# Moving the second mixer's eight modulation slots into the two feed-forward blocks before and after it

## The chip, the cores and the metric

The kernel runs on one core of one Trainium2 chip. The metric is the device time of one execution in microseconds; three runs are given by their median and their ends. One more execution was recorded by the hardware profiler, and all rows of the profile come from that one.

The engines are named as in the profile: PE is TensorE's matmul, PEld its weight load, DVE is VectorE, ACT is ScalarE, POOL is GpSimd, SP is the queue that issues most loads from HBM.

## The reference, cut to what matters

The model is a chain of three transformer layers over 512 latent tokens (and 256 context tokens, in the first two), width 1024, all in float32. Each layer is a mixer (attention beside a pooling and a convolution branch in the first two layers, attention beside a linear recurrence in the third) followed by a gated feed-forward block. Every layer is steered by a modulation vector that depends on the condition vectors `c` and `c_ctx` alone, not on the tokens:

```python
def adaln(cond, w_mod, b_mod):
    m = jnp.dot(jax.nn.silu(cond), w_mod) + b_mod
    return jnp.split(m[..., None, :], 6, axis=-1)
...
sh1, sc1, g1, sh2, sc2, g2 = adaln(c, w_mod[l], b_mod[l])
h = modulate(rms_norm(x, norm1_g[l]), sh1, sc1)
...
x = x + g1 * jnp.einsum('blm,md->bld', mix, w_out[l])
x = x + g2 * swiglu(modulate(rms_norm(x, norm2_g[l]), sh2, sc2), w_ffn_in[l], w_ffn_out[l])
```

`w_mod` is 1024 by 6144 for each layer, so the three modulations read 72 MB and hold 6 parts (two shifts, two scales, two gates) of 1024 numbers for each of two conditions. A layer's parts are needed at different times: the first shift and scale at its first norm, the first gate at the mixer's output projection, the second shift and scale at the norm before the feed-forward block, and the second gate inside that block.

## The kernel before, in words

**Slots.** The modulation work is cut into 72 slots, 24 for each layer, of 256 columns of `w_mod` each. They are used in one fixed order, the list `mods` (all slots of layer 0, then of layer 1, then of layer 2); this text counts them from 0 to 71. `mod_slot` is one of them. It takes 1 MB of weights, which `Weights.next` loads in two halves of 512 KB into buffers named `raw`. Eight calls of matmul (line 343; each appears in the profile as two records, so a slot has 16) multiply the conditions with the weights, 32 columns of the array at a time, into a PSUM tile. Then `post` copies the tile to SBUF on ACT (line 349), and `post2` transposes it twice on PE (line 354) into another PSUM tile, reduces that on DVE (line 356), and adds bias and gain on DVE (lines 358 and 362). `mod_slot` gets a tag that says which PSUM banks it takes: "pj" (two banks, shared with the projections) in the mixers, "ap" (two other banks) in the feed-forward blocks. Ahead of the first slot of layer 2, which is slot 48, `cond` (line 332) computes the conditions of that layer on ACT.

**Where the slots are issued.** Eight slots go with the start of the first mixer. `MODS_MIX` says how many each of the first two mixers issues within its windows (lists of work items that `windows` writes out and `layer` spreads over the steps of the attention); `MODS_FFN` says how many follow each of the 22 hidden blocks of a feed-forward block in `ffn`, through `mod_fill`. Before, that is 12 slots in the first mixer (8 to 19), 22 in the first feed-forward block (20 to 41, one to a hidden block), 8 in the second mixer (42 to 49), and 22 in the second feed-forward block (50 to 71). The third feed-forward block has none.

**Weights.** All other weights come through a second stream of the same class. A load of 1 MB comes in two halves into the same `raw` buffers, of which there are four; each half is then split into a high part (`whi`, ACT, line 229) and a low part (`wlo`, POOL, line 230). Both streams load one entry ahead of the one in use. So a slot whose weights are there, but which has not run, holds two of the four `raw` buffers.

**Matmuls.** Each projection is three matmuls for one product (lines 254, 257 and 258 in `mm3`). A hidden block of a feed-forward block is 16 such triples of 512 columns (in the first one also 16 of 256 columns for the context), then an ACT Silu (line 953), a product on DVE (line 954) and a split.

**The mixer's other work.** In the second mixer DVE runs 62 taps of a convolution over 512 columns (line 664, `conv_taps`), the maxima of the softmax (line 799), its weighted difference (line 844) and parts of the pooling branch (lines 639 to 644). PE transposes queries and keys (line 791, in `qk_turn`) into a "pj" bank, from an operand that POOL finishes (line 782). `conv_ln` normalises the convolution: sums on PE (lines 676 and 306), a power on POOL (line 297), a spread on PE (line 322).

**Order.** The program is written in one order, and the framework's scheduler sorts each engine's queue by the written order and its own estimate of times. On the chip each engine runs its queue in that order.

Of the kernel before, what the change touches and what calls it, by code (L numbers as in the profile page):

```python
# [24 lines left out]
NJ = FF // 128  # L25
# [216 lines left out]
class K:  # L242
# [463 lines left out]
        return post(g, ps)  # L706


    MODS_MIX = [(4, 8, 0, 0), (2, 4, 2, 0)]
    MODS_FFN = [[1] * NJ, [1] * NJ, [0] * NJ]  # L710

    LAST = [(0, 0, 0.2, 0.4, 0.6, 0.8, 1), (0, 0.1, 0.4, 0.7, 1)]
    SLOT = {"g": 0, "u": 1, "p": 2, "v0": 3, "q0": 4, "q1": 5, "v1": 6, "q2": 7, "q3": 8}
# [1 line left out]
    def windows(self, l):  # L715
# [22 lines left out]
        q0, v0 = tm("q0"), tm("v0")  # L738
        nm = self.MODS_MIX[l]
        conv = [it for g in ("01", "2") for n in "gu" for it in fm(n) if it[2] in g]  # L740
# [180 lines left out]
    def ffn(self, l, pf, hx, hc, xt, xc, then, at=None):  # L921
# [5 lines left out]
        for gi, (j0, jn, cn) in enumerate(DOWN[l]):  # L927
            gt = []
            for j in range(j0, j0 + jn):
# [28 lines left out]
                gt.append((gh, gl))  # L958
                self.mod_fill(self.MODS_FFN[l][j], "ap", j == j0 + jn - 1)
                if at and j in at:  # L960
# [788 lines left out]
```

## Time and profile before

| | us |
|---|---|
| median of 3 runs | 2637.24 |
| lowest and highest | 2633.56, 2638.14 |
| the profiled execution, its own time | 2634.79 |
| its span, first to last instruction | 2632.9 |
| PE busy in it | 2500.2 (95%) |
| DVE, ACT, POOL busy in it | 954.6, 907.7, 1143.8 |

The profiled execution is 2.45 us below the median of the runs and lies within them. Times within it are counted from the span's start. The first mixer ends and the first feed-forward block begins near 460 us; the second mixer lies from about 1030 to 1390 us, the second feed-forward block from there to about 1775 us, and the third one from about 2255 us to the end.

Matmuls are pipelined, so one record is longer than the step from one start to the next; a busy PE in a stretch says that it never waited, not how fast it went.

### The profile page before, as it was taken

The page shows a single profiled execution, that of the slowest core. Times are in us where ns is not written, and L with a number is a line of the kernel's source. Part 1 is how long each engine was busy: PE and PEld are TensorE (multiplying, and loading weights), DVE is VectorE, ACT ScalarE, POOL GpSimd, SP SyncE. Part 2 cuts the span into 40 slices and gives each one's busy share as a digit, 9 for nine tenths or more (in the row PEclk, how much of TensorE's full clock was granted, in tenths as well). Part 3 has the DMA queues.
Part 4 walks back from the last instruction along what each step waited for, and adds up shares of the span by engine and source line. Part 5 has one row for each costly group of instructions (what it writes and reads, how often), then busy time and mean ns, then how long its engine had stood idle before and what let it go on. Part 6 is the DMA issues. An engine that isn't in the chain of part 4 may idle for free.

```text
span 2632.9 us, 38646 instructions
## 1 busy us (share of the span) xinstructions
PE 2500.2 (95%) x15840; PEld 2131.1 (81%) x15840; DVE 954.6 (36%) x1932; ACT 907.7 (34%) x1905; POOL 1143.8 (43%) x965
## 2 busy tenths in 40 slices
PE   7889989999999999999999999999998898999998
PEld 5778869988888889877788777778887788888887
DVE  4896464121120123488542112113322756210112
ACT  4334543322122124333534223234443543422222
POOL 4544324433333334655326545454322344555553
PEclk9889989999999999999999999999998999999999
DMA  7113311323323233222324435343111021222221
GB/s 253 50 49 110 116 72 40 121 81 113 96 96 102 91 99 101 78 65 81 97 80 145 160 128 160 120 160 104 49 33 51 17 97 49 81 96 97 96 92 53
DMA packets 68961, 248.55 MB, mean 94 GB/s; under 512 B 7472, under 2 KB 10800, under 8 KB 67120
## 3 DMA queue, kind: packets, MB, share of 16 engines
q1 hardware_dynamic: 64992, 231.11, 26.9%
q10 hardware_dynamic: 3792, 14.97, 1.5%
q8 instruction: 125, 2.05, 0.3%
q14 instruction: 52, 0.43, 0.0%
HBM read 239.75 MB, written 6.29 MB: 93 GB/s over the span
## 4 chain that ended last, share of the span: by engine, by line
PE 48%; DVE 5%; ACT 2%; POOL 2%; issue 1%; DMA 1%; POOLq 0%; DVEq 0%; ACTq 0%
PE s2t L254 6%; PE s2t L258 6%; PE s2t L257 6%; PE pj L254 5%; PE pj L257 5%; PE pj L258 5%; PE ap L819 2%; DVE mix L664 1%; PE ap L254 1%; PE ap L257 1%; PE ap L258 1%; POOL wlo L230 1%; PE s2t L1531 1%; PE s2t L836 1%; PE ap L343 1%
## 5 line engine op out<-in xcount | busy, mean ns | idle before, releaser
L230 POOL TENSOR_TENSOR wlo<-raw,whi 128x512 fp32r<-128x512 f32 x576 | 745.4, 1326 | 700.5 <-ACT whi L229 700.2
L229 ACT CAST whi<-raw 128x512 fp32r<-128x512 f32 x576 | 319.5, 615 | 675.2 <-PE pj L257 248.1
L254 PE MATMUL s2t<-hh,whi 128*128 128x512 f32 (+1 forms) x1184 | 448.9, 380 | 0.8 <-ACT whi L229 0.8
L257 PE MATMUL s2t<-hl,whi 128*128 128x512 f32 (+1 forms) x1184 | 446.2, 377 | 1.8 <-POOL hl L428 1.8
L258 PE MATMUL s2t<-hh,wlo 128*128 128x512 f32 (+1 forms) x1184 | 447.5, 378 | 0.1
L254 PE MATMUL pj<-hh,whi 128*128 128x256 f32 (+1 forms) x1088 | 337.2, 312 | 8.5 <-ACT hh L425 2.9
L257 PE MATMUL pj<-hl,whi 128*128 128x256 f32 (+1 forms) x1088 | 331.5, 305 | 3.5 <-DVE hl L430 2.4
L258 PE MATMUL pj<-hh,wlo 128*128 128x256 f32 (+1 forms) x1088 | 331.1, 305 | 0.3 <-POOL wlo L230 0.3
L954 DVE TENSOR_TENSOR sg<-sg,s2t 128x512 f32<-128x512 f32 x66 | 45.4, 688 | 651.8 <-ACT sg L953 651.8
L257 PEld LDWEIGHTS s2t<-hl,whi 128*128 128x128 f32 x1184 | 223.0, 189 | 47.0 <-POOL hl L428 2.9
L258 PEld LDWEIGHTS s2t<-hh,wlo 128*128 128x128 f32 x1184 | 223.1, 188 | 46.9 <-issue 1.2
L254 PEld LDWEIGHTS s2t<-hh,whi 128*128 128x128 f32 x1184 | 222.4, 188 | 46.3 <-issue 2.1
L254 PEld LDWEIGHTS pj<-hh,whi 128*128 128x128 f32 x1088 | 210.4, 194 | 25.1 <-ACT hh L425 4.0
L327 POOL TENSOR_TENSOR gl<-sg,gh 128x512 fp32r<-128x512 f32 (+1 forms) x66 | 97.7, 1481 | 293.4 <-ACT gh L326 293.4
L257 PEld LDWEIGHTS pj<-hl,whi 128*128 128x128 f32 x1088 | 211.0, 194 | 12.4 <-DVE hl L430 2.6
L258 PEld LDWEIGHTS pj<-hh,wlo 128*128 128x128 f32 x1088 | 209.6, 193 | 8.5 <-POOL wlo L230 0.5
L254 PE MATMUL pj<-whi,hh 128*128 128x256 f32 x672 | 196.9, 293 | 1.3 <-ACT v L699 0.9
L257 PE MATMUL pj<-wlo,hh 128*128 128x256 f32 x672 | 194.4, 289 | 0.0
L258 PE MATMUL pj<-whi,hl 128*128 128x256 f32 x672 | 193.9, 289 | 0.0
L893 DVE SCALAR_TENSOR_TENSOR xt<-pj,mod,xt 128x256 f32<-128x256 f32 x224 | 101.6, 480 | 175.6 <-PE pj L258 175.1
L258 PE MATMUL pj<-gh,wlo 128*128 128x512 f32 (+1 forms) x400 | 145.6, 364 | 0.0
L254 PE MATMUL pj<-gh,whi 128*128 128x512 f32 (+1 forms) x400 | 145.5, 366 | 0.0
(382 smaller groups left out, 4464.7 us busy)
## 6 DMA issues: line engine op xcount, KB each, us to landing
raw<-in_w_mod SPq DMA_DIRECT2D x144, 512.0 KB, 4.0
raw<-in_w_up SPq DMA_DIRECT2D x132, 512.0 KB, 3.9
raw<-in_w_dn SPq DMA_DIRECT2D x66, 512.0 KB, 4.0
raw<-in_w_in SPq DMA_DIRECT2D x60, 512.0 KB, 3.9
raw<-in_w_out SPq DMA_DIRECT2D x24, 512.0 KB, 3.9
xt<-xs ACTq DMA_DIRECT2D x4, 1024.0 KB, 5.7
xt<-in_xT ACTq DMA_DIRECT2D x2, 1024.0 KB, 7.9
xs<-xt SPq DMA_DIRECT2D x2, 1024.0 KB, 3.8
```

What stands on the lines that cost most here:

```text
L229: nc.scalar.copy(out=h, in_=raw[:, q])
L230: nc.gpsimd.tensor_tensor(out=lo[:, s][:, q], in0=raw[:, q], in1=h.bitcast(F32), op=ALU.subtract)
L254: i = mm(ps, lhsT=lh, rhs=rh, start=start, stop=False)
L257: mm(ps, lhsT=lh, rhs=rl, start=False, stop=False)
L258: return mm(ps, lhsT=ll, rhs=rh, start=False, stop=stop)
L327: (lo_eng or self.nc.vector).tensor_tensor(out=lo, in0=src, in1=hi.bitcast(F32), op=ALU.subtract)
L343: nc.tensor.matmul(ps[g:g + 32], lhsT=self.cond_t[:, k, :], rhs=raw[k // 4][:, k % 4, :], start=k < 4, stop=k >= 4, tile_position=(0, g))
L664: nc.vector.scalar_tensor_tensor(out=m, in0=u[:, j:j + W], scalar=dw(j), in1=m, op0=ALU.mult, op1=ALU.add)
L819: i = nc.tensor.matmul(o, lhsT=at[:, j], rhs=v[:, j0 + j, :], start=j0 + j == 0, stop=j0 + j == nj - 1)
L836: nc.tensor.matmul(s[c][:, k0:k1], lhsT=qk[r, 0, a, t], rhs=qk[r, 1, b, k0:k1], start=n == 0, stop=n == 2)
L893: self.nc.vector.scalar_tensor_tensor(out=x, in0=ps, scalar=col, in1=x, op0=ALU.mult, op1=ALU.add)
L954: nc.vector.tensor_tensor(out=sg[:, c], in0=sg[:, c], in1=p[:, 1], op=ALU.mult)
```

## The change

Two tables are changed, and nothing else:

```diff
-    MODS_MIX = [(4, 8, 0, 0), (2, 4, 2, 0)]
-    MODS_FFN = [[1] * NJ, [1] * NJ, [0] * NJ]
+    MODS_MIX = [(4, 8, 0, 0), (0, 0, 0, 0)]
+    MODS_FFN = [[2] * 6 + [1] * (NJ - 6), [2] * 2 + [1] * (NJ - 2), [0] * NJ]
```

`NJ` is 22. The second mixer issues no slot any more. The first feed-forward block issues 28 slots (20 to 47) instead of 22, two behind each of its first six hidden blocks; the second one issues 24 (48 to 71) instead of 22, two behind each of its first two. So slots 42 to 47 are issued earlier, slots 48 and 49 later, and slots 50 to 71 at about their old places. The conditions of layer 2, which `cond` computes ahead of slot 48, move from the second mixer to the second feed-forward block.

## Rows read from the trace of the kernel before

**Rows 1.** The page's first part: busy us, share of the span, instructions.
```profile
PE 2500.2 (95%) x15840; PEld 2131.1 (81%) x15840; DVE 954.6 (36%) x1932; ACT 907.7 (34%) x1905; POOL 1143.8 (43%) x965
```

**Rows 2.** Busy time by stretch: feed-forward blocks 1, 2, 3, then the second mixer.
```profile
core 0: us, PE busy (x) PEld busy (x) DVE busy (x) ACT busy (x) POOL busy (x), PEclk, DMA share, GB/s
500.00:1000.00 500.00, 499.21 (x3025) 421.06 (x3024) 85.86 (x200) 102.65 (x188) 175.95 (x131) 1.00 0.30 99
1420.00:1770.00 350.00, 349.95 (x1748) 269.63 (x1747) 49.44 (x125) 100.75 (x186) 174.07 (x140) 1.00 0.44 144
2300.00:2550.00 250.00, 250.00 (x1073) 201.08 (x1073) 25.18 (x51) 63.61 (x116) 128.68 (x102) 1.00 0.28 93
...
1149.00:1228.00 79.00, 66.76 (x504) 57.59 (x502) 77.32 (x130) 29.12 (x67) 48.15 (x34) 0.93 0.21 68
1228.00:1300.00 72.00, 71.46 (x560) 60.17 (x560) 37.36 (x75) 29.94 (x71) 27.36 (x22) 0.98 0.27 88
```

**Rows 3.** Timeline of ACT, second feed-forward block: start, length, engine, line.
```profile
1440.11 0.60 ACT L953 ACTIVATE sg<-s2t 128x512 f32<-128x512 f32 x1 [5.71 <-PE s2t L258]
...
1452.68 0.60 ACT L953 ACTIVATE sg<-s2t 128x512 f32<-128x512 f32 x1 [4.95 <-PE s2t L258]
```

**Rows 4.** The same view of the third feed-forward block.
```profile
2302.85 0.59 ACT L953 ACTIVATE sg<-s2t 128x512 f32<-128x512 f32 x1
...
2314.05 0.59 ACT L953 ACTIVATE sg<-s2t 128x512 f32<-128x512 f32 x1
```

**Rows 5.** Timeline of PE around one slot of the second feed-forward block.
```profile
1452.20 0.39 PE L258 MATMUL s2t<-hh,wlo 128*128 128x512 f32 x1
1452.52 1.07 PE L343 MATMUL ap<-raw,cond 128*32 128x256 f32 x16
1453.52 0.44 PE L354 MATMUL ap<-ident,ev 128*128 128x128 f32 x2
1453.71 0.48 PE L254 MATMUL s2t<-hh,whi 128*128 128x512 f32 x1
1454.03 0.40 PE L257 MATMUL s2t<-hl,whi 128*128 128x512 f32 x1
```

**Rows 6.** DVE's instructions on the modulation tile, by stretch (busy, count).
```profile
1149.00:1228.00 79.00, 1.94 (x7) 0.00 (x0) 0.93 0.21 68
```

**Rows 7.** The chain that ended last from 1149 to 1228 us, by line.
```profile
by line: DVE mix L664 42.4%; DVE e L844 9.7%; DVE nmx L799 9.0%; DVE sq L779 6.8%; DVE edge L639 3.6%; DVE nm L765 3.2%; DVE ss L762 3.1%; POOL rsy L297 2.8%; DVE up L641 2.7%; DVE up L644 2.6%; issue 2.5%; DVE qk L327 2.5%; DVE ray L860 1.
```

**Rows 8.** The same chain from 1228 to 1300 us.
```profile
by line: PE pj L254 16.8%; PE pj L257 16.5%; PE pj L258 16.4%; PE s2t L836 12.4%; PE ap L819 11.8%; PE pj L343 7.1%; PE ap L815 5.7%; DMA raw<-in_w_out 5.4%; PE pj L791 3.0%; PE pj L676 2.8%; ACT at L817 1.2%; PE ap L867 1.2%; DVE qk L327 1
```

**Rows 9.** PE's waits, 1149 to 1310 us: us in total, times, longest.
```profile
PE pj L791 <- DVE mod L356: 5.9, 1, 5.9
PE pj L254 <- DVE qk L327: 2.7, 1, 2.7
PE pj L322 <- POOL rsy L297: 2.1, 1, 2.1
```

**Rows 10.** Timeline of PE around the longest of these waits.
```profile
1221.86 0.44 PE L354 MATMUL pj<-ident,ev 128*128 128x128 f32 x2 [0.48 <-DVE qk L327]
1228.15 1.09 PE L791 MATMUL pj<-ident,y 128*128 128x128 f32 x4 [5.85 <-DVE mod L356]
```

**Rows 11.** Timeline of DVE in the same place.
```profile
1226.74 1.19 DVE L644 COPY up<-edge 64x8 f32<-64x8 f32 x2
1227.85 0.16 DVE L356 TENSOR_REDUCE mod<-pj 128x4 f32<-128x16 f32 x1
```

**Rows 12.** Timeline of POOL in the same place.
```profile
1222.35 1.26 POOL L782 TENSOR_TENSOR y<-y,sq 128x512 f32<-128x512 f32 x1
```

**Rows 13.** Two stretches of the second mixer at a lower clock (columns as in Rows 2).
```profile
1176.23:1179.64 3.41, 2.99 (x15) 2.69 (x13) 3.41 (x8) 0.37 (x1) 1.83 (x2) 0.50 0.00 0
...
1224.02:1230.85 6.83, 2.70 (x13) 2.73 (x14) 6.63 (x16) 1.18 (x3) 6.13 (x5) 0.50 0.09 22
```

**Rows 14.** Timeline of PE at the mixer's last two slots.
```profile
1298.50 1.07 PE L343 MATMUL pj<-raw,cond 128*32 128x256 f32 x16
```

**Rows 15.** Timeline of DVE, the sums of the convolution's norm.
```profile
1304.22 0.16 DVE L296 TENSOR_SCALAR rsv<-pj 128x4 f32<-128x4 f32 x1 [0.93 <-PE pj L306]
```

**Rows 16.** Timeline of POOL behind it.
```profile
1303.79 2.51 POOL L230 TENSOR_TENSOR wlo<-raw,whi 128x512 fp32r<-128x512 f32 x2 [3.24 <-ACT whi L229]
1306.25 1.02 POOL L297 TENSOR_TENSOR rsy<-rsv,mhalf 128x4 f32<-128x4 f32 x1
```

**Rows 17.** Timeline of ACT where the conditions of layer 2 are computed.
```profile
1271.03 1.28 ACT L332 ACT_TABLE_LOAD   x1
```

**Rows 18.** Timeline of SP in the first feed-forward block.
```profile
591.65 2.81 SPq L218 DMA_DIRECT2D raw<-in_w_mod  x2
602.51 0.80 SPq L226 DMA_DIRECT2D raw<-in_w_up  x2
```

**Rows 19.** The page's DMA issues: KB each, median us from issue to landing.
```profile
raw<-in_w_mod SPq DMA_DIRECT2D x144, 512.0 KB, 4.0
```

## The prediction

> **What bounds the kernel now.** I read the page first: PE is busy for 95% of the span [rows 1], so the question is where PE waits, and whether the eight slots stand there or where it never waits. The table of busy time by stretch answers that for the two kinds of place. In the feed-forward blocks PE is busy for 499.21 of 500, 349.95 of 350 and 250.00 of 250 us at the full clock [rows 2]: whatever is put there comes on top. In the second mixer it is not so. From 1149 to 1228 us PE is busy for 66.76 of 79 us while DVE is busy for 77.32, and from 1228 to 1300 us PE is busy for 71.46 of 72 [rows 2]. The chain of waits, read next, says the same: in the first of these stretches it runs over DVE, 42.4% of it over the convolution's taps [rows 7], in the second over PE [rows 8]. So the change moves work from a place where only a part of it costs time to one where all of it does. What can repay that is the waits that the slots themselves cause in the mixer, so I read PE's waits there last [rows 9].
>
> **What a slot costs in a feed-forward block.** The Silu of one hidden block follows that of the block before by 1452.68 - 1440.11 = 12.57 us in the second feed-forward block, with one slot to a hidden block [rows 3], and by 2314.05 - 2302.85 = 11.20 us in the third, which has none [rows 4]. The difference, 1.37 us, is a slot. The timeline of PE gives the same from inside: from the last matmul ahead of the slot to the second one behind it 1454.03 - 1452.20 = 1.83 us pass where two steps of the hidden block's 11.20 / 48 = 0.233 us would take 0.47, so 1.36 us are the slot's [rows 5]. Its copy on ACT and its small sums on DVE lie beside the matmuls, where ACT and DVE are busy for 100.75 and 49.44 of 350 us [rows 2].
>
> All eight become the second slot behind a hidden block. For them I bound the price from below by 1.2 us: a step of 0.32 instead of 0.233 us stands on either side of the slot [rows 5], and two slots in a row would share one pair. I take the full 1.37 us for all eight, since the transposes of one slot may come between, so the feed-forward blocks grow by 8 x 1.37 = 11.0 us; by the lower bound it is 9.6. From above the price is open only if PE waits for a slot's weights; that is a rival below.
>
> The loads move too: 16 halves of 512 KB go past SP's queue earlier (12) or later (4). They take 4.0 us from issue to landing [rows 19] and the DMA share is 0.30 in the first feed-forward block [rows 2], so bandwidth covers them. What is scarce is the `raw` buffers. Now the load for the next slot goes out at 591.65, and the next hidden block's weights at 602.51, when a slot's matmuls have begun to give their buffers back [rows 18]. With two slots the second one's load takes the buffers that the weights' split frees, and the weights wait for a slot's matmuls. A load with its split takes some 9 us (4.0 to land, and four pieces of POOL at 2.51 / 2 = 1.26 us each [rows 16]), less than the second feed-forward block's 12.57 us to a hidden block [rows 3], and the first one's hidden blocks are longer by the context, so I cost this at nothing. If that cover is gone, PE waits.
>
> The computing of the conditions, with a table load of 1.28 us on ACT [rows 17] and another behind it to go back, leaves the mixer, where PE was the chain [rows 8], and goes to the second feed-forward block, whose Silu needs that table anyway. I cost it at nothing either way; from both sides it is bounded by the two loads, 2.6 us.
>
> **What the mixer gives back.** Five terms, in order of time.
>
> First, in the stretch bound by DVE the slots' own DVE instructions take 1.94 us [rows 6]. The slots' PE time there returns nothing, since PE waits for DVE anyway. Return 1.9 us.
>
> Second, the longest wait of PE in the mixer is the slots' own. At 1228.15 the transposes of line 791 start after 5.85 us of waiting for the reduce of slot 44 [rows 10], because it holds the "pj" bank that they need. The reduce is ready to run at about 1222.3, after the slot's transposes, but stands in DVE's queue behind the softmax and the pooling, and runs at 1227.85 [rows 11]. The transposes' operand was finished by POOL at 1222.35 + 1.26 = 1223.61 [rows 12]. Without the slot they can start there: 1228.15 - 1223.6 = 4.5 us. Its bounds are nothing, if the next user of a bank inherits the wait, and the whole 5.85.
>
> Third, that wait lowered the clock: from 1224.02 to 1230.85 the granted clock is 0.50 of full speed, 1.2 GHz, and PE is busy for 2.70 us of it [rows 13]. At 2.4 GHz that work takes half, so 1.35 us come back with the second term, and none without it.
>
> Fourth, in the stretch bound by PE the slots' matmuls are 7.1% of the chain's 72 us [rows 8], 5.1 us for five slots. The last of them, at 1298.50 [rows 14], stands in front of the convolution's norm, where PE waits for other engines right after, so I leave it out: 5.1 - 1.07 = 4.0, and for the transposes of the other four 4 x (1.37 - 1.07) = 1.2. Return 5.2 us; bounds nothing (the attention's latency binds at once) and 5 x 1.37 = 6.9.
>
> Fifth, the last slot's matmuls free the buffers for a load of the output weights, whose split runs on POOL at 1303.79 and holds up the power of the convolution's norm to 1306.25, though its operand is there at 1304.22 + 0.16 [rows 15, 16]. PE waits 2.1 us for that power [rows 9]. Without the slot the load goes out earlier. Between 0 and 1306.25 - 1304.38 = 1.9 us; I take 1.0.
>
> **The sum.** 11.0 - (1.9 + 4.5 + 1.35 + 5.2 + 1.0) = 11.0 - 13.95 = -3.0 us. Against the profiled execution's own 2634.79 that is 2631.8; the median of the runs is 2.45 us above that execution, and the same step from it gives 2634.2. I predict 2634. With all low bounds together (the mixer returns only DVE's 1.9) the change costs 9.1 us; with all high ones it gains 1.9 + 5.85 + 1.35 + 6.9 + 1.9 - 9.6 = 8.3.
>
> **Rivals.** *The bank wait is inherited.* DVE's queue is just as full without the slot, and the transposes, or the projection behind them, may wait for another bank whose reader stands behind the same pooling. For it speaks that PE also waits 2.7 us for DVE's line 327 with a projection [rows 9]; against it, that line 791's operand is there by 1223.61. Terms two and three fall out: -3.0 + 5.85 = +2.9, 2640.
>
> *The slots were cover, and the mixer keeps its length.* This is the one on the other side. Its place is from 1228 to 1300 us: without the slots PE has 6.9 us less to do there, and if it then waits for the softmax instead, terms two to five are lost or filled with waiting: +11.0 - 1.9 = +9.1, 2646. The clock adds to it. Each time PE has waited for long in this mixer the granted clock has gone to 0.50, 1.2 GHz, as after the 2.7 us wait and in the 5.85 us one [rows 9, 13]; another stretch like the second of these would cost 1.35 us more. It decides from the point where more than about 3 of the 13.95 us are not returned. The Trainium skill states the same danger as a rule (TensorE: Matmul & The Clock Gate, "Why this matters for your kernels"): keep the engine free of idle gaps between bursts of matmuls, or its clock falls back. By that rule taking fillers out of a mixer is a loss, and the time would be that of this rival, 2646 or a little more; the trace agrees that idle lowers the clock, but also shows that the worst gap hangs on a filler. Against the rival speaks that PE is busy for 71.46 of 72 us there, with projections enough to fill.
>
> *The slots take more with them.* The scheduler lays out every queue anew, and all waits near slots may go: 8 x 1.37 = 11.0 of PE time, 5.9 + 2.7 + 2.1 = 10.7 of waits [rows 9], and half of 2.70 + 2.99 us of work at the low clock [rows 13], 2.8: together 24.5 for 11.0, so -13.5, 2624. For it: the 2.7 us wait also comes with a slot holding a "pj" bank. Against it: DVE's queue is full there, so PE would reach the next wait sooner.
>
> *The second slot's weights come late.* In the first six hidden blocks the buffers allow no more than one slot ahead; if a load is issued less than 4.0 us before its matmuls, PE waits for the rest. For two such waits of 4.0 us: -3.0 + 8 = +5, 2642; more of them, more. Against it: the scheduler may put the slot anywhere in the next hidden block.
>
> **How the numbers follow.** A difference of 0.2%, 5.3 us, is about what a measurement of this kernel can tell from no change. My forecast, -8 to +3 around -3.0, gets 0.44, the inherited wait 0.20, the cover 0.14, more taken along 0.14, late weights 0.08. Of the forecast's 0.44 I put 0.16 beyond -5.3, 0.26 within, 0.02 above; of the inherited wait 0.14 within and 0.06 above; of the late weights 0.02 and 0.06. Faster: 0.16 + 0.14 = 0.30. Slower: 0.02 + 0.06 + 0.14 + 0.06 = 0.28. Within: 0.42. Both signs hold much, so the forecast's own range is 2629 to 2640; the range for all cases is 2623 to 2647, from the case where more is taken along to that where the slots were cover.
>
> **What would show it.** In the profile after: 28 and 24 groups of 16 records of line 343 in the first two feed-forward blocks and none in the second mixer; hidden blocks with two slots that are 1.2 to 1.4 us longer than their neighbours, and PE still busy throughout; no wait of line 791 for DVE's line 356, and no stretch at half clock near 1230 us; the second mixer shorter by about 14 us. Wrong would be: a PE wait on line 343 for DMA (late weights); line 791 or 254 waiting as long for another reader on DVE (inherited); PE's busy share below 95% in the 70 us behind DVE's stretch (cover).

## The result and the profile after

The changed kernel takes 2653.58 us (median of 5 runs, 2652.19 to 2662.63), the kernel before beside it 2638.14 (5 runs): a ratio of 1.0065, 95% interval 1.0041 to 1.0089. In a second set (6 runs, labelled a2 below) it took 2650.84 against 2634.13, 1.0060 (1.0045 to 1.0076). So it is slower, by about 16 us, where -3 was forecast. The profiled execution shown here is the slowest of its five (span 2660.8 us); where a size matters, the profile of a2 (span 2651.9) and a second one of the kernel before (b2, span 2633.4) stand beside it.

Page after, first part, for [rows 1]:

```profile
PE 2509.5 (94%) x15840; PEld 2141.6 (80%) x15840; DVE 956.2 (36%) x1932; ACT 904.8 (34%) x1903; POOL 1145.7 (43%) x965
```

PE's 15840 instructions are the same number as before, and its share falls to 94%: it now waits more. Where, the busy time by stretch tells (after; columns as in [rows 2]): the three feed-forward blocks, then the 91 us that end with PE's longest wait in the second mixer, and the 72 us behind it.

```profile
500.00:1000.00 500.00, 498.93 (x3068) 419.32 (x3067) 85.35 (x211) 102.34 (x190) 175.11 (x131) 1.00 0.34 109
1430.00:1776.00 346.00, 346.00 (x1745) 267.20 (x1743) 52.26 (x129) 99.42 (x185) 173.60 (x139) 1.00 0.46 148
2340.00:2600.00 260.00, 260.00 (x1116) 209.23 (x1115) 30.09 (x62) 67.18 (x123) 134.27 (x107) 1.00 0.29 93
...
1158.00:1249.00 91.00, 68.07 (x505) 62.72 (x505) 85.45 (x136) 31.79 (x73) 52.71 (x35) 0.90 0.10 30
1249.00:1321.00 72.00, 66.64 (x484) 60.16 (x483) 32.49 (x64) 29.27 (x70) 28.74 (x24) 0.95 0.11 37
```

The feed-forward blocks are as full as they were. The mixer is not: behind the long wait PE is busy for 66.64 of 72 us, 93%, where it was 71.46 of 72 [rows 2], and in front of it DVE is again busy nearly all the time.

**The feed-forward blocks.** Timeline of ACT, the first and the seventh Silu of the first block, before and then after:

```profile
481.23 0.59 ACT L953 ACTIVATE sg<-s2t 128x512 f32<-128x512 f32 x1
...
620.19 0.60 ACT L953 ACTIVATE sg<-s2t 128x512 f32<-128x512 f32 x1 [10.75 <-PE s2t L258]
```

```profile
481.62 0.59 ACT L953 ACTIVATE sg<-s2t 128x512 f32<-128x512 f32 x1
...
628.67 0.60 ACT L953 ACTIVATE sg<-s2t 128x512 f32<-128x512 f32 x1 [8.57 <-PE s2t L258]
```

138.96 us became 147.05: six slots more in six hidden blocks, 8.09 us, 1.35 each. From the first to the last Silu of the block it is 532.89 and 541.25. In the feed-forward blocks PE waits for a slot's weights in one place only, at slots 48 and 49 (what PE's line 343 sat idle for from 1405 to 1420 us, after; us, times):

```profile
  DMA raw<-in_w_mod: 0.6, 2
```

**The second mixer.** PE's waits from the first block's last Silu to the tenth Silu of the second block, after (us in total, times, longest):

```profile
PE pj L791 <- DVE qk L327: 13.3, 2, 11.5
PE pj L791 <- POOL y L782: 12.6, 5, 3.8
PE ap L819 <- ACT at L817: 6.5, 6, 2.3
```

The second of these in the kernel before, in the same stretch:

```profile
PE pj L791 <- POOL y L782: 4.0, 3, 2.2
```

The wait for the slot's reduce [rows 9, 10] is gone. The same instruction, the transposes of line 791, now waits twice as long, and the view puts that down to another reader of a "pj" bank; its waits for its operand, which POOL's line 782 finishes, rose from 4.0 to 12.6 us besides. Timeline of PE there, after:

```profile
1236.06 0.94 PE L819 MATMUL ap<-v,at 128*128 128x128 f32 x6 [1.81 <-ACT at L817]
1248.49 1.09 PE L791 MATMUL pj<-ident,y 128*128 128x128 f32 x4 [11.50 <-DVE qk L327]
```

And of DVE, which holds it:

```profile
1235.51 1.54 DVE L765 TENSOR_TENSOR nm<-y,rsy 128x512 f32<-128x512 f32 x1 [0.90 <-POOL rsy L297]
1237.08 1.84 DVE L779 TENSOR_TENSOR sq<-nm,sg 128x256 f32<-128x256 f32 x2
1238.84 1.30 DVE L639 TENSOR_TENSOR edge<-uc,PV 64x8 f32<-64x8 f32 x2
...
1242.57 1.82 DVE L641 SCALAR_TENSOR_TENSOR up<-uc,PV,up 64x512 f32<-64x512 f32 x1
1244.32 1.00 DVE L844 SCALAR_TENSOR_TENSOR e<-e,rr 128x768 f32<-128x768 f32 x1
1245.25 1.29 DVE L644 COPY up<-edge 64x8 f32<-64x8 f32 x2
...
1247.92 0.42 DVE L327 TENSOR_TENSOR qk<-pj,qk 128x256 fp32r<-128x256 f32 x1
```

The split of the previous query and key group, line 327, takes 0.42 us and frees the bank, but stands behind 12 us of normalization, pooling and softmax. It is the place of [rows 11], with another instruction at the end of the same queue. In a2 the wait is 11.49 us.

The bank is only half of that wait. POOL finished the transposes' operand at 1241.38 + 1.26 = 1242.64:

```profile
1241.38 1.26 POOL L782 TENSOR_TENSOR y<-y,sq 128x512 f32<-128x512 f32 x1
```

PE stood idle from 1248.49 - 11.50 = 1236.99. For the first 5.65 us the operand was not there, and the bank alone cost the other 5.85. Before, the operand was missing for the first 1.3 us of the wait [rows 10, 12] and the bank cost 4.5. So most of what the wait grew by is the operand, which goes through DVE's lines 765 and 779 above.

**Where the time went.** For each stretch I split PE's time in three: idle; what it lost to the clock, half of its busy time while the granted clock was 0.50; and the rest, its work at full clock. The second mixer is counted from the last Silu of the first feed-forward block to the tenth of the second, so its column holds the two slots added there; the third from the 21st Silu of the second block to the fifth of the third block. All in us, from the profiled executions, "length = work + idle + clock" up to rounding; the split is worked out from the traces and stands in no view as it is:

| kernel | block 1 | second mixer | third mixer |
|---|---|---|---|
| before | 532.9 | 546.2 = 508.4 + 29.5 + 8.3 | 546.2 = 493.3 + 38.0 + 14.9 |
| b2 (before) | 533.1 | 553.4 = 507.5 + 29.0 + 16.9 | 546.2 = 493.6 + 37.7 + 14.9 |
| after | 541.2 | 557.1 = 496.2 + 42.8 + 18.1 | 555.7 = 492.8 + 41.9 + 21.0 |
| a2 (after) | 541.0 | 548.8 = 496.6 + 41.5 + 10.8 | 552.1 = 492.8 + 39.8 + 19.5 |

Three things are to be seen (a kernel's two profiles averaged). In the second mixer PE's work fell by 11.5 us, 14.2 with the two added slots taken out at 1.35 each, as much as the forecast wanted back in all and more than 8 x 1.37 = 11.0; but its idle time rose by 12.9. The waits for the operand of line 791 rose by as much: 4.0 + 1.3 us before, 12.6 + 5.65 after. The third mixer, in which not an instruction is changed, takes 6 to 10 us more, most of it at the low clock. And two executions of the kernel before differ by 7.2 us in the second mixer, all of it the clock (8.3 and 16.9), though their spans are 2632.9 and 2633.4.

The lines behind two of the rows, busy time by stretch of the second and the third mixer, before and after:

```profile
1014.12:1560.30 546.18, 516.71 (x3594) 447.00 (x3597) 256.84 (x497) 217.56 (x483) 273.07 (x240) 0.98 0.30 101
...
1756.62:2302.85 546.23, 508.21 (x3349) 445.69 (x3342) 223.46 (x433) 238.55 (x466) 217.18 (x191) 0.97 0.20 65
```

```profile
1022.87:1579.96 557.09, 514.31 (x3486) 451.12 (x3489) 255.14 (x481) 212.73 (x474) 273.17 (x240) 0.95 0.27 87
...
1776.20:2331.93 555.73, 513.83 (x3349) 450.74 (x3342) 225.23 (x433) 238.67 (x465) 218.06 (x191) 0.96 0.20 64
```

PE's count falls by 108 in the second mixer, six slots of 18 records (eight out, two in), and is the same in the third, 3349. What differs in the third is the order, and that by little: the first 371 PE records and the first 185 of DVE's 433 stand as before, and of those behind them some 80 and 14 stand in another place. Two profiles of one kernel agree in it, so the scheduler has changed the order there too.

### The profile page after: what moved, and what is told of

Same layout as the page of the kernel before. It is cut to its first block, busy times and chain, and to the rows that moved or that the text cites. A ratio compares the mean times of both kernels' runs of the same rounds, so it can differ in the third digit from the quotient of the medians.

```text
span 2660.8 us, 38654 instructions
## 1 busy us (share of the span) xinstructions
PE 2509.5 (94%) x15840; PEld 2141.6 (80%) x15840; DVE 956.2 (36%) x1932; ACT 904.8 (34%) x1903; POOL 1145.7 (43%) x965
## 4 chain that ended last, share of the span: by engine, by line
PE 45%; DVE 5%; ACT 2%; POOL 2%; issue 1%; DMA 1%; POOLq 0%; DVEq 0%; ACTq 0%
PE s2t L254 6%; PE s2t L258 6%; PE s2t L257 6%; PE pj L254 5%; PE pj L257 5%; PE pj L258 5%; PE ap L819 1%; PE ap L254 1%; PE ap L257 1%; PE ap L258 1%; PE s2t L1531 1%; POOL wlo L230 1%; PE ap L343 1%; PE s L254 1%; PE s L257 1%
```

## The experiments

Ratios are to the kernel before on the same chip, with their 95% intervals; times of different experiments can come from different chips, so small differences between them are better taken from the ratios. Sizes of stages are split as in the table, from one profile each.

**Both again.** The changed kernel and the kernel before, unedited (a2 above, and b2).

> The changed kernel unaltered, timed again beside the kernel before, and profiled a second time, since one profile can't tell what a stage costs from what this execution's clock did. All theories: 2649 to 2656 us; the feed-forward blocks again 8.2 and 2.7 us longer, the wait of PE before a transpose of line 791 for DVE's line 327 again 11 to 12 us, since the queues' order is fixed when the kernel is built. Only the stretches at the low clock may lie elsewhere; if their sum in the second mixer falls from 51 us to under 35, the mixer is 6 us or more shorter than in the first profile of this kernel.

> The kernel before unaltered, for a second profile. The waits of PE should be those of the first profile (5.9 us before line 791); stretches at the low clock may differ, and with them the lengths of the three mixers by several us each, while the feed-forward blocks agree within 0.5 us.

Measured: 1.0060 (1.0045 to 1.0076), and 2635.17 us for one run of the kernel before. The loss stands, and the second mixer is 8.3 us shorter in a2 than in the first profile, most of it the clock, as was held possible.

**The slots' places kept as empty items.** The scheduler's windows are as before, with nothing in the places of the slots.

```diff
-    MODS_MIX = [(4, 8, 0, 0), (0, 0, 0, 0)]
+    MODS_MIX = [(4, 8, 0, 0), (2, 4, 2, 0)]
...
-                        return self.mod_slot(*self.mods.pop(0))
+                        return self.mod_slot(*self.mods.pop(0)) if full else [(0, lambda: None), (1, lambda: None)]
```

> The changed kernel, but the second mixer's windows keep an empty item where each of its eight slots stood, with the slot's two stages and its cost of 1.0 in the written order's clock; so every other item is written where it was before the change, and only the slots' own instructions are gone. Theory A (the shifted written order is the cause: without the eight items the projections, pooling and convolution items come at other steps of the attention, and DVE's queue is laid out worse): the mixer gives back what was forecast, about 14 us against 11 in the feed-forward blocks, so 2632 to 2638 us, and the longest PE wait of the mixer is under 4 us. Theory B (the slots were cover: with their PE work gone PE reaches the same full DVE queue sooner and waits there, wherever the items are written): within 5 us of the changed kernel, 2649 to 2658, with a PE wait of 8 us or more for DVE's line 327 before a transpose of line 791.

Measured: 2643.7 us, 1.0028 (1.0016 to 1.0041), 7 below the changed kernel with the same work in it, and between the ranges of the two theories. The second mixer is 546.2 = 496.8 + 37.5 + 11.9, the third 544.0. PE's longest wait in the mixer is 6.0 us and for POOL's line 782; the waits for line 327 are 1.9 us in all. So neither theory is borne out.

**The eight slots left out.** This kernel does not compute slots 42 to 49 at all; the parts of the modulation that they would fill are set to one, so its output is not the reference's.

```diff
-        if (l, s) == (2, 0):
+        if (l, s) == (2, 1):
...
+        for m in self.MOD[1:]:
+            nc.vector.memset(m, 1.0)
...
+        del self.mods[42:50]
...
+    MODS_FFN = [[1] * NJ, [1] * NJ, [0] * NJ]
```

> Slots 42 to 49 are left out altogether (their columns of the modulation of layers 1 and 2 are set to one and never computed, so the output is not the reference's); the feed-forward blocks issue 22 and 22 slots as before the change and the mixer none. This takes the price in the feed-forward blocks off the changed kernel. If the feed-forward blocks charge 1.37 us for a slot, it is 11 us below the changed kernel, 2642 to 2643, and still 3 to 6 us above the kernel before, although it does 8 slots less: then the mixer alone got slower (both theories). If the mixer had given back what was forecast, it would be 14 us below the kernel before, 2624.

Measured: 2635.88 us, 1.0001 (0.9984 to 1.0017). Taking eight slots out of the mixer and putting them nowhere saves nothing that can be measured, in this one order; it is neither the 2642 of both theories nor the 2624 of a mixer that gives back what was forecast. The second mixer is 546.9 = 497.1 + 38.0 + 11.7: the work is gone, and the idle time is 8.5 to 9 us above the two profiles of before.

**Two of the slots moved, and the other six.**

```diff
-    MODS_MIX = [(4, 8, 0, 0), (2, 4, 2, 0)]
-    MODS_FFN = [[1] * NJ, [1] * NJ, [0] * NJ]
+    MODS_MIX = [(4, 8, 0, 0), (2, 4, 0, 0)]
+    MODS_FFN = [[1] * NJ, [2] * 2 + [1] * (NJ - 2), [0] * NJ]
```

> Only the mixer's last two slots (48 and 49, with the conditions of layer 2) move, into the second feed-forward block; the six others stay. Theory A and B alike: the feed-forward block charges 2.7 us; the two slots stood behind DVE's full stretch, so their going should not touch the wait at the transpose of line 791, and the whole is within 5 us of the kernel before, 2633 to 2643. If it comes out as slow as the changed kernel, the cause lies in the last window, the pooling and the convolution's norm, not in DVE's full stretch.

```diff
+    MODS_MIX = [(4, 8, 0, 0), (0, 0, 2, 0)]
+    MODS_FFN = [[2] * 6 + [1] * (NJ - 6), [1] * NJ, [0] * NJ]
```

> Only the mixer's first six slots (42 to 47) move, into the first feed-forward block; slots 48 and 49 stay in the third window. The feed-forward block charges 8.2 to 8.8 us. Theory A and B: the harm is done in the first three windows, so it is nearly as slow as the changed kernel, 2648 to 2655, with the long wait of PE at line 791. If the cause lies in the third window (its pooling items, which the last two slots displaced), it is within 8 us of the kernel before, 2638 to 2646.

Measured: 2639.03, 1.0010 (0.9996 to 1.0024), for the two; 2644.77, 1.0038 (1.0023 to 1.0052), for the six. The two came out as expected. The six fell below their 2648 to 2655: by the rule set down for them the cause would lie in the third window, and the orders tried below show that one such pair cannot tell. With the six alone block 1 takes 541.1, the second mixer 556.3 = 496.8 + 38.6 + 20.9, and the third mixer 546.6, as before.

**The turn brought forward.** The transposes of a query and key group with their split (`qk_turn`: lines 791 and 327) get a higher priority, so that line 327 stands ahead of the last pooling.

```diff
+        def turn():
+            with self.tc.high_priority(800 if l == 1 else 1):
+                self.qk_turn(l, g, y, qk)
+        return [(0, lambda: self.qk_norm(l, g, ps, y, tables)), (10, turn)]
```

> The changed kernel, but in the second mixer the transposes of queries and keys and their split (lines 791, 326 and 327) are scheduled with a raised priority, so that the split for head 2 stands in DVE's queue ahead of the last two groups of the pooling's small operations instead of behind them. Theory B1 (the loss in the mixer is the bank wait that another reader inherited): the 11.5 us wait falls below 4 us, the clock does not fall there, and the whole is 7 us or more below the changed kernel, 2640 to 2647. Theory B2 (DVE's full queue sets the end of that stretch whatever stands first): the wait only moves to another PE instruction, and the whole stays within 4 us of the changed kernel.

Measured: 2643.23, 1.0035 (1.0021 to 1.0048). The 11.5 us wait is gone. This form also raised the first mixer's turns by one step, and PE's idle time there rose from 54.2 us before to 61.9. So it was run again for the second mixer alone:

```diff
+        if l == 0:
+            return [(0, lambda: self.qk_norm(l, g, ps, y, tables)), (10, lambda: self.qk_turn(l, g, y, qk))]
...
+            with self.tc.high_priority(800):
```

> The changed kernel with the raised priority in the second mixer alone. In the first try the other two layers' turns had been raised by one step too, and the first mixer's idle time on PE had risen from 52 to 55 us to 62. Theory 'the inherited bank wait is worth about 7.5 us': this kernel is 7.5 us below the changed kernel, and 2 to 3 more below for the first mixer, 2640 to 2644, a ratio of 1.001 to 1.003. Rival 'the first try's gain was a draw of the order': anywhere in the scatter of the orders without slots in the mixer, 2643 to 2652, 1.0028 to 1.006.

Measured: 2642.78, 1.0030 (1.0018 to 1.0042). Its second mixer is 541.6 = 497.5 + 33.2 + 10.9. Of its waits on PE from 1137 to 1420 us the two longest groups are these (lines are 8 higher there):

```profile
PE ap L875 <- DVE on L870: 9.8, 3, 7.8
PE pj L799 <- POOL y L790: 9.8, 3, 4.5
```

The wait for the split has left; others of up to 7.8 us have taken a part of its place, and the transposes still wait 9.8 us for their operand. The time lies in the range of the theory, but its ratio lies in that of the rival too, so this run does not tell the price of the wait from a draw of the order.

**Work in the empty places.** The kernel with the empty items, and in each of them eight matmuls of a slot's shape into a "pj" bank that nobody reads.

```diff
+    def filler(self):
+        ps = self.ps([128, 256])
+        for k in range(KD):
+            g = 32 * (k % 4)
+            self.nc.tensor.matmul(ps[g:g + 32], lhsT=self.cond_t[:, k, :], rhs=self.PW,
+                                  start=k < 4, stop=k >= 4, tile_position=(0, g))
...
+                        return self.mod_slot(*self.mods.pop(0)) if full else self.filler()
```

> As the kernel with the empty items, but each of the mixer's eight places now issues the slot's eight matmuls on weights that lie in SBUF anyway, into a PSUM bank that nobody reads: PE work of 1.07 us each without load, copy, transposes or DVE work (pure extra work, the output is unaffected). Theory cover (PE waits for DVE there, and the work fills the waits and keeps the clock up): within 3 us of the kernel with the empty items, or faster. Rival (PE's time counts): 6 to 9 us slower than that kernel, 2649 to 2653.

Measured: 2653.75, 1.0078 (1.0061 to 1.0094), 10 us more than with empty items (13 by the ratios), with 11.1 us more work in the second mixer (507.9) and 2.9 less idle. So in this pair PE's time is not free: work that comes in costs nearly its length. The fillers also take a "pj" bank each and change the queues' order, and what they cost apart from that is not shown.

**All eight into the first block.**

```diff
+    MODS_FFN = [[2] * 8 + [1] * (NJ - 8), [1] * NJ, [0] * NJ]
```

> All eight extra slots stand behind the first eight hidden blocks of the first feed-forward block (30, 22 and 20 then); the second mixer has none, as in the changed kernel, and the second feed-forward block is as in the kernel before. Theory 'the third mixer pays for a new order': its 6 to 9 us more come from the order of its queues, which the two slots in the second feed-forward block changed. Here that order should be the one of the kernel before, so the third mixer should take 546 to 547 us (552 to 556 in the changed kernel), the first feed-forward block 532.9 + 8 x 1.37 = 543.9, the second mixer what it takes in the changed kernel, and the total should be some 5 us below the changed kernel: 2644 to 2647, a ratio of 1.003 to 1.005. Rival 'the third mixer pays for what ran before it, whatever its order' (the clock): the third mixer takes 550 or more and the time is that of the changed kernel, 1.006.

Measured: 2646.94, 1.0043 (1.0028 to 1.0058). Block 1 is 543.9: eight slots cost 11.0 us, to the tenth what was forecast. The third mixer took 548.4, where 546 to 547 were expected from the old order; but its queues stand record for record as in the changed kernel, not as before. Same order, 552.1 to 555.7 there and 548.4 here.

Then three kernels without a new edit: this one with the turn brought forward in the first form and in the second, and the one with the empty items with the first form.

> The kernel with all eight extra slots in the first feed-forward block, and the second mixer's transposes with their splits (the turn of a query and key group) issued with a higher priority on top. If the inherited bank wait and the third mixer's order are two separate terms they add up: 7.5 us less than the changed kernel for the wait and 5 less for the order, so 2637 to 2641, a ratio of 1.000 to 1.003. Rival, that the raised priority worked only by giving the third mixer back some time (it took 549.3 there): then the two overlap and the time stays at 2643 or above, 1.0035.

> All eight extra slots in the first feed-forward block, with the raised priority in the second mixer alone. If the raise brings the second mixer to the 539 us that it took in the first try, and the first mixer stays at 480: 2638 to 2642, a ratio of 1.001 to 1.0025. Rival, a draw of the order: 2643 to 2652.

> The changed kernel with the slots' places kept as empty items in the mixer, and the raised priority on top. With the places kept PE waits for the turn's split only 1.9 us in all, its longest wait (6.0) is for POOL. So the raised priority should bring at most 1.9: 2641 to 2644, a ratio of 1.002 to 1.003. Rival, that both edits do the same by another way (a turn is brought forward) and more of it helps: 2638 or less.

Measured: 2644.83, 1.0028 (1.0017 to 1.0040); 2640.59, 1.0015 (1.0001 to 1.0029); 2651.84, 1.0059 (1.0042 to 1.0075). Only the second lies in the range expected; the two terms of the first do not add up, and the third is 8 us above its range. The first two have the shortest second mixers of all, 538.9 and 539.4. The third lost 8 us by what gained 8 in the changed kernel: against the empty items alone its second mixer is 553.5 instead of 546.2.

**The order of the kernel before changed, and nothing else.** First the turns raised as in the first form, then the eight slots in other windows of the same mixer, then the two pooling items swapped; that last edit in the changed kernel too.

> The kernel before with the same raised priority for the second mixer's turns. Theory 'the turn waits behind the pooling only where the slots are gone': here PE's longest wait hangs on a slot's reduce and only 2.7 us on the turn's split, so at most 2.7 us come back and the time is 2632 to 2636, a ratio of 0.999 to 1.000. Rival 'the turns are late in any case': the wait falls as it does without slots, 5 us or more, a ratio of 0.998 or below, and this kernel would beat both.

```diff
-    MODS_MIX = [(4, 8, 0, 0), (2, 4, 2, 0)]
+    MODS_MIX = [(4, 8, 0, 0), (4, 4, 0, 0)]
```

> The kernel before, with the second mixer's eight slots laid 4, 4, 0 and 0 over its four windows (they were 2, 4, 2 and 0); the feed-forward blocks are as before. No work is added, removed or taken out of the mixer; only the order of the queues is another. Theory 'the slots are what counts': all eight still stand in the mixer, so the time is that of the kernel before within 0.2%, 2631 to 2641. Rival 'the order is what counts' (each new layout of the queues costs some us, whatever is in it): 2643 to 2650, a ratio of 1.003 to 1.005, as raising the turns did.

```diff
+    MODS_MIX = [(4, 8, 0, 0), (2, 3, 3, 0)]
```

> The same with the eight slots laid 2, 3, 3 and 0 over the windows, the smallest step from the kernel before. 'The slots are what counts': 2631 to 2641. 'The order is what counts': 2643 to 2650; smaller than with 4, 4, 0 and 0 if it goes by how much of the order changes.

```diff
-            merge(tm("q3") + [("pool", 0), ("pool", 1)] +
+            merge(tm("q3") + ([("pool", 0), ("pool", 1)] if l == 0 else [("pool", 1), ("pool", 0)]) +
```

> The kernel before with the two pooling items of the second mixer issued in the opposite order, another change of order alone. 'The slots are what counts': 2631 to 2641. 'The order is what counts': 2643 to 2650.

> The changed kernel with the same two pooling items in the opposite order. If orders scatter by some us around a mean that the slots' place sets, this falls anywhere between 2643 and 2655, the range of the six orders tried without slots in the mixer. Then the means over orders tell the price of the move: 'the slots are what counts' puts the orders with slots in the mixer at 2636 to 2640 on average and those without at 2646 to 2650, some 10 us apart; 'the order is what counts' puts both averages within 4 us of each other.

Measured: turns raised 2645.96, 1.0032 (1.0018 to 1.0045); slots 4, 4, 0, 0: 2650.89, 1.0055 (1.0043 to 1.0068); slots 2, 3, 3, 0: 2639.6, 1.0014 (1.0004 to 1.0025); pools swapped 2639.93, 1.0020 (1.0005 to 1.0035); pools swapped in the changed kernel 2648.13, 1.0050 (1.0037 to 1.0064). Turns raised missed both its ranges, 2632 to 2636 and below; its idle time in the first mixer, 62.3 us, rose as with the turns raised above. Laying the same eight slots 4, 4, 0, 0 over the same mixer costs almost what moving them out costs, where "the slots are what counts" had 2631 to 2641; the other two orders with the slots in the mixer lie in that range. Busy time of that kernel's second mixer:

```profile
1011.47:1571.48 560.01, 527.97 (x3594) 454.59 (x3597) 255.27 (x497) 217.40 (x482) 269.79 (x240) 0.96 0.30 98
```

560.0 = 509.2 + 32.0 + 18.8, with all its slots in place; and its third mixer took 551.0.

**Over the orders.** With the slots in the mixer five orders were run, the kernel before among them at 1.0000: their ratios average 1.0024, with a standard deviation of 0.0021. With the eight moved there are nine (the changed kernel at 1.0062, empty items, both forms of the turn, eight in block 1 alone and with both forms, empty items with the turn, pools swapped): they average 1.0039, with 0.0016. The difference is 0.0015, 3.9 us, with a standard error of 0.0011 (the root of 0.0021² / 5 + 0.0016² / 9), 2.8 us. That is between the 10 us of "the slots are what counts" and nothing, and is told safely from neither; the -3 of the forecast lies 2.5 errors below it. The orders were not drawn at random, some are built on others, so the error is a rough one; without the four kernels that raise the first mixer's turns too the difference is 0.0016. No kernel tried beats the kernel before.

The second mixer over the same orders, by the split of the table: 553.2 = 505.8 + 31.5 + 15.9 on average with the slots in it, 543.9 = 495.0 + 36.4 + 12.5 without them (the two added slots taken out where they stand in it). So eight slots take 10.8 us of PE work with them, their 8 x 1.37, and 4.9 us come back as idle time; the mixer is 9.3 us shorter, with a standard error of 2.6. The 14.2 and the 12.9 us of the first pair are the high work and the low idle time of one order: with the slots in the mixer the work went from 502.2 to 509.2 us, and the kernel before has 508 of it and the least idle time of the five.

## Why the prediction was wrong

**The price in the feed-forward blocks: right.** 11.0 us forecast, 11.0 measured with all eight in block 1; 8.1 for the six of the changed kernel. The full 1.37 us, and not the lower bound of 1.2, was the one to take for second slots.

**Late weights: costed at nothing, and rightly.** Two waits of 0.6 us in all. The rival with two waits of 4.0 us is out.

**The conditions: nothing either way.** No wait of theirs shows among the longest of the mixer or of the second block.

**The mixer's PE work: came back in full.** The fourth term and what the first did not count give 14.2 us of work at full clock in the first pair, 10.8 over the orders, where 5.2 were booked for it. What failed is the other half of the term, that PE would use the time: 4.9 us over the orders, 12.9 in the first pair, came back as waiting.

**The bank wait: the step that failed.** The second term booked 4.5 us, on the ground that without the slot's reduce the transposes could start when their operand is there. The bank's part did not go. Line 327, the reader of the first rival, holds it for 5.85 us where the reduce held it for 4.5. And PE came to the transposes ahead of their operand: the waits for it rose from 5.3 to 18.2 us. That PE did so because it had less to do is argued, not shown. Neither the term nor the rival had that. The rival priced the inherited wait at +5.85 because it let only the old wait live on, and what spoke against it, an operand ready by 1223.61, held for the old order alone. With the longer wait the third term turned around: the stretch at half clock around the wait is 17.07 us long where it was 6.83 [rows 13], and PE is busy for 5.72 us of it instead of 2.70.

```profile
1134.74:1141.57 6.83, 6.83 (x30) 6.36 (x30) 2.42 (x7) 2.35 (x5) 1.50 (x2) 0.50 0.49 156
...
1237.14:1254.21 17.07, 5.72 (x28) 5.52 (x28) 15.97 (x30) 4.01 (x10) 13.43 (x10) 0.50 0.19 61
```

With line 327 ahead of the pooling the changed kernel is some 8 us faster, with the second mixer at 541.4 and 541.6 us. But the same raise gained 2 and 6 us (by the medians) with all eight slots in block 1, and lost 8 on the empty items and 10 on the kernel before (the 2 and the two losses with the first mixer's turns raised too). So a price of the wait by itself is not shown. A wait in such a mixer is not a sum to be taken off; when it goes, the next one moves up.

**The first and fifth terms.** DVE has no instruction on the slots left there, yet from its first tap to the end of that wait it takes 1247.92 + 0.42 - 1141.2 = 107.1 us, where it took 1227.85 + 0.16 - 1126.7 = 101.3 [rows 11]: the 1.9 us were not returned. The fifth term came true, and more: the wait of 2.1 us for the power of the convolution's norm [rows 9], of which I had taken 1.0, is gone (0.0 us after, 0.1 in a2); whether the earlier load did it is not shown. The wait for line 297 that is left, 0.6 us at another norm near 1408 us, stands in the kernel before too.

**The cover rival: half borne out.** Its sign is there, PE at 93% behind the long wait, and leaving the slots out altogether saves nothing (1.0001). But if they had stood in idle time, fillers in their places would have been free, and in the one pair tried they cost 10 us. Over the orders idle time takes back 4.9 of 10.8 us, a little under half. What fits all of this, though no run shows it alone, is that each layout of the queues has its own waits, and the kernel before has the best of the five orders tried with its work.

**What the forecast lacked.** It took every queue as it stood, minus the slots. The scheduler lays all of them out anew, and the third mixer with them. Eleven profiles have its queues in the changed kernel's order (one PE record apart in one of them), three of them with all eight slots still in the second mixer (turns raised; 4, 4, 0, 0; 2, 3, 3, 0): it takes 547.8 to 555.7 us in them, 547.8 to 551.2 in those three, against 546.2 to 550.1 in the three that keep the old order (before twice, and, one PE record apart, slots left out). Two more that keep DVE's queue as it was (the six alone, the pooling items swapped) take 546.6 and 546.7. So a longer third mixer needs no slot moved. Some 3 us go with the order (averages 550.4 and 547.5); the rest, up to 8 us between executions of one and the same order, is the clock for the most part (14.2 to 21.0 us lost), and what decides it is open.

The forecast put the third mixer and the draw of an order at nothing, without a reason. So of the measured 16 us some 4, with an error of 3, are the price of the move over orders, 11 spent and about 7 returned; the rest is the order that the changed kernel happened to get, set against the best one. My range (2623 to 2647) left this draw out. It is worth 0.0016 to 0.0021 of the time in either group, 4 to 5.5 us, more than the 3 that the whole change was forecast to bring. Why an order is good or bad, beyond the waits shown, stays open.

## What to carry to other kernels

Work put into a block that PE fills costs its full length and can be priced to a tenth of a us; what it frees in a stretch with many waits cannot be read off the waits one by one, because the next reader of the same bank stands in the same queue, and the instruction that waited may come to find its operand missing instead. Where a scheduler lays out the queues, add to the range the scatter that a few edits of order alone give, and look for it in stages that the edit doesn't touch. One order against one order tells little about a move of this size: compare several of each before the move itself is judged.

## What the runs showed of the hardware

The granted clock falls in places where PE had not waited. After 14.74 us in which it was busy for 14.74 at full clock (busy time by stretch, after) it went to 0.50, 1.2 GHz, for the 6.83 us shown above, busy for all of them:

```profile
1120.00:1134.74 14.74, 14.74 (x103) 12.63 (x102) 4.05 (x9) 5.39 (x13) 3.49 (x3) 1.00 0.05 17
```

PE's last wait ahead of it, 0.59 us, ended at 1115.29. The fall is real: the step between projection matmuls of 128x256 is 0.12 us ahead of it and 0.21 us in it. In the last 4 us ahead of it such matmuls take turns with those of line 836, which use 64 of the array's 128 rows; what decided it is open.

The Trainium skill (TensorE: Matmul & The Clock Gate, "Why this matters for your kernels") asks for no idle gaps between bursts, so that the clock stays up. The 17.07 us around the long wait agree with it; keeping to it was not enough for this stretch, which has no gap in the 14.74 us in front of it.

The lows also fall differently in executions of the same kernel: 8.3 and 16.9 us were lost in the second mixer of the kernel before, 18.1 and 10.8 in that of the changed one. In the kernel before most of the difference is one stretch: in b2 the clock is at 0.50 for 13.7 us from 1133.9 us, with PE busy ahead of it and through it, and in the other profile it does not fall there. In the third mixer of the kernel before the two profiles agree to 0.1 us in length and in what the clock took.
